# Expert layers of a two-layer decoder: one gather and one residual write per group of eight experts, where there was one per four

## The chip, the cores and the metric

The kernel runs on one core of one Trainium2 chip. The metric is the device time of one execution in microseconds (us), of which the median over runs is taken. The engines are named as the profile names them: PE (matrix products), DVE and ACT (elementwise work), POOL, and SP, which here issues nearly all transfers. Transfers from memory run on the core's 16 DMA engines.

## What is computed

The reference is a trunk of two layers over 528 rows (16 meta tokens and 512 tokens) of width 1024, in float32. Layer 0 is a gated short convolution, layer 1 latent attention, and behind each stands a mixture of experts, added to the residual `h`:

```
grp    = argmax(xf @ w_grp)                      # one of 8 groups per token
top_i  = the best 2 of the group's 8 experts     # 64 experts in all
gate   = p_group * p_expert / sum(p_expert)
hh     = silu(xb @ w_gate[e]) * (xb @ w_up[e])   # 1024 -> 256
ys     = hh @ w_down[e]                          # 256 -> 1024
y      = sum over a token's two experts of ys * gate
h      = h + y
```

Each expert has three matrices of 1 MB (1024x256, 1024x256, 256x1024), so a layer's 64 experts are 192 MB of weights, and every one is read once.

## The kernel before

**Quads.** The experts of a layer are taken four at a time. Such a *quad* (16 a layer, 0 to 15) has 128 slots, 32 for each expert (`CAP`), which lie on the 128 partitions; two quads make a group. `Moe.run` walks over the quads, and `quad` (L663) writes the PE's work out by hand in this order:

- `gate_up(q, gu, xT, 0)` and `(…, 1)` (L573): the four experts' gate products and up products, 64 PE records each, with `combined` of the quad before it between and behind them (L667, L671);
- `gather` for the quad to come (L532): a 0/1 matrix `dr` that `select_scaled` builds on DVE (slots by tokens, times the row's norm) multiplies `h`, in float32: 5 token tiles (4 in layer 1, which has no meta tokens) times two halves of 512 columns;
- `scatter` (L552): a small product that tells each slot its token and its gate;
- `turn` (L582): silu on ACT, a product on DVE, two transposes; `turned` (L543): eight transposes of the gathered rows, which give `xT` of the next quad;
- `down` (L594): the down products in two halves; `split_scaled` (L213) puts gate times result into a high and a low part, and `combine_part` (L645) multiplies both by the 0/1 matrix `DT` (tokens by slots, from `back`, L565) and adds the product to `h`, tile by tile, on DVE (L651).

The first gather of a layer is another: `first_gather` (L419) makes `xT` straight away with `h` as the stationary operand, eight products of 128 columns for each token tile.

**The ring.** All weights come through one ring of 1 MB slots (`Ring`, L67). The order of the loads is fixed, SP issues them one by one, and each waits until the slot's former load was released: `gate_up` releases four slots a call, `down` four. Slots are of four kinds: A (4), B (5 in layer 0, 9 in layer 1, `NB`), K and R together (13 and 10, `NR`), and X (3 and 4, `NX`). K and R, on the right of the memory, serve loads up to the first of quad `LATE` (12 in layer 0, 15 in layer 1). At that quad `late_work` (L653) gives their memory up, runs a loop for experts with over 32 tokens (its count is zero for these inputs; the engines jump over it), starts what is wanted for the next stage (in layer 1 the load and spreading of the last norm's weights, L1272 to L1276), and opens the X slots.

So the order is set by hand on PE, by the ring on SP, and by the scheduler, which follows the order of the calls, on DVE and ACT.

## Time and profile before

| what | value |
|---|---|
| median of 3 runs | 1456.99 us (1456.9 to 1458.02) |
| the profiled execution's own time | 1459.79 us |
| its span, first to last instruction | 1458.0 us |
| PE busy | 1349.8 us, 93% |
| DVE, ACT busy | 661.4 us, 305.0 us |
| data moved | 438.14 MB, mean 301 GB/s |

The span holds five stages: the convolution layer and first routing (to 265 us), the experts of layer 0 (265 to 750), attention (750 to 986), the experts of layer 1 (986 to about 1445), and the last norm with the output. In the page's digits each place is a fortieth of the span (36.45 us), 9 is 90% or more. A wait counts where it stands ahead of the instruction that ends last; a busy PE may be working on something whose end nobody waits for yet.

### The profile page before, as it was taken

Reading aid. Unit: us, or ns where it says so; the run is one execution under the profiler, and the core shown is the slowest. Engines: PE = TensorE matmul, PEld = TensorE weight load, DVE = VectorE, ACT = ScalarE, POOL = GpSimd, SP = SyncE. Lnnn points to the kernel's source line nnn. Section 1 sums busy time; section 2 is a strip of 40 time slices with the busy share of each in tenths; the row PEclk is TensorE's granted clock in tenths of the full one; section 3 lists DMA queues with packets and bytes.
Section 4 is the critical chain, followed back from the end, with each engine's and each line's share of the span. In section 5 each row is a group of like instructions: output and inputs, shape, how many; then the busy total and the mean of one; then the engine's idle time right before and its main releaser. Section 6 shows DMA issues by size and latency. Waiting matters only on the chain. (4 is left out here: it accounts for less than half of the span.)

```text
span 1458.0 us, 23499 instructions
## 1 busy us (share of the span) xinstructions
PE 1349.8 (93%) x9847; PEld 843.9 (58%) x9847; DVE 661.4 (45%) x1495; ACT 305.0 (21%) x665; POOL 50.6 (3%) x131
## 2 busy tenths in 40 slices
PE   6999999999999999988989999999999989888966
PEld 6999758644444444433458888895454444443422
DVE  4555325444344434443455676544444433433334
ACT  6333112100101000120134675421111100101002
POOL 1011101000000000000011000000000000000001
PEclk9999998999999999999999999999999999999987
DMA  8322534699999999479950002968999999999982
GB/s 300 145 89 95 228 146 174 248 414 416 420 420 419 420 420 419 182 290 423 416 212 26 30 30 87 363 252 340 419 419 419 419 419 419 419 419 419 419 322 81
DMA packets 66854, 438.14 MB, mean 301 GB/s; under 512 B 8353, under 2 KB 8737, under 8 KB 16178
## 3 DMA queue, kind: packets, MB, share of 16 engines
q1 hardware_dynamic: 65008, 435.79, 73.5%
q8 instruction: 81, 1.33, 0.4%
q10 hardware_dynamic: 1730, 0.74, 0.2%
q14 instruction: 35, 0.29, 0.1%
HBM read 434.40 MB, written 2.10 MB: 299 GB/s over the span
## 5 line engine op out<-in xcount | busy, mean ns | idle before, releaser
L539 PE MATMUL w<-h,dr 128*128 128x512 f32 x480 | 218.0, 602 | 0.0
L651 DVE TENSOR_TENSOR h<-h,w 128x512 f32<-128x512 f32 x256 | 158.9, 682 | 122.7 <-PE w L649 122.7
L649 PE MATMUL w<-y,DT 128*128 128x512 f32 x576 | 166.5, 423 | 7.4 <-ACT y L214 3.4
L539 PEld LDWEIGHTS w<-h,dr 128*128 128x128 f32 x480 | 87.5, 190 | 116.4 <-issue 105.9
L577 PE MATMUL gu<-B,xT 128*32 128x256 f32 x1456 | 129.4, 400 | 20.6 <-issue 12.7
L649 PEld LDWEIGHTS w<-y,DT 128*128 128x128 f32 x576 | 90.8, 179 | 82.8 <-DVE h L651 31.6
L577 PE MATMUL gu<-R,xT 128*32 128x256 f32 x1648 | 124.0, 386 | 4.5 <-DMA R<-in_w_up_dram 3.7
L214 ACT ACTIVATE y<-dn,gs 128x512 fp32r<-128x512 f32 x64 | 44.0, 688 | 363.8 <-PE w L649 202.5
L522 DVE TENSOR_TENSOR dr<-rm,cs 128x640 f32<-128x640 f32 (+1 forms) x30 | 22.7, 758 | 191.7 <-PE w L539 191.7
L577 PEld LDWEIGHTS gu<-B,xT 128*32 128x32 f32 x1456 | 62.9, 115 | 65.1 <-issue 31.6
L577 PE MATMUL gu<-A,xT 128*32 128x256 f32 x640 | 82.5, 405 | 17.1 <-DMA A<-in_w_up_dram 11.6
L540 ACT ACTIVATE xg<-w 128x512 f32<-128x512 f32 x60 | 35.9, 598 | 277.7 <-PE w L539 277.7
L577 PEld LDWEIGHTS gu<-R,xT 128*32 128x32 f32 x1648 | 63.1, 111 | 47.3 <-issue 12.4
L867 PE MATMUL acc<-xH,wL 128*128 128x264 f32 x384 | 79.0, 286 | 0.0
L867 PE MATMUL acc<-xL,wH 128*128 128x264 f32 x384 | 78.3, 284 | 0.2 <-DVE xL L211 0.2
L867 PE MATMUL acc<-xH,wH 128*128 128x264 f32 x384 | 78.1, 284 | 0.1
L585 DVE TENSOR_TENSOR sg<-sg,gu 128x256 f32<-128x256 f32 x32 | 13.5, 421 | 134.6 <-ACT sg L584 134.6
L215 DVE SCALAR_TENSOR_TENSOR y<-dn,gs,y 128x512 fp32r<-128x512 f32 x64 | 47.7, 746 | 53.6 <-ACT y L214 53.5
L606 PE MATMUL dn<-A,sg 128*32 128x512 f32 x272 | 67.7, 674 | 2.9 <-DVE sg L591 2.9
L606 PE MATMUL dn<-R,sg 128*32 128x512 f32 x344 | 63.4, 682 | 2.9 <-DVE sg L591 2.8
L214 ACT ACTIVATE wH<-A,gc 128x256 fp32r<-128x256 f32 (+1 forms) x119 | 52.7, 521 | 61.7 <-PE acc L867 37.0
L577 PEld LDWEIGHTS gu<-A,xT 128*32 128x32 f32 x640 | 38.5, 117 | 44.3 <-DMA A<-in_w_up_dram 15.4
(348 smaller groups left out, 2154.7 us busy)
## 6 DMA issues: line engine op xcount, KB each, us to landing
R<-in_w_up_dram SPq DMA_DIRECT2D x55, 1024.0 KB, 19.9
B<-in_w_gate_dram SPq DMA_DIRECT2D x51, 1024.0 KB, 19.9
R<-in_w_gate_dram SPq DMA_DIRECT2D x48, 1024.0 KB, 19.9
R<-in_w_down_dram SPq DMA_DIRECT2D x43, 1024.0 KB, 14.1
B<-in_w_up_dram SPq DMA_DIRECT2D x40, 1024.0 KB, 19.8
A<-in_w_down_dram SPq DMA_DIRECT2D x32, 1024.0 KB, 18.1
B<-in_w_down_dram SPq DMA_DIRECT2D x31, 1024.0 KB, 19.9
A<-in_w_up_dram SPq DMA_DIRECT2D x22, 1024.0 KB, 19.9
```

Source lines behind the costliest of these rows:

```text
L214: i = A.activation(H, src, AF.Copy, scale=g)
L215: return i, V.scalar_tensor_tensor(L, src, g, H.bitcast(F32), op0=ALU.mult, op1=ALU.subtract)
L522: V.tensor_tensor(d.rearrange("p t (e s) -> p t e s", e=4), self.rm0[:, :, 4 * q:4 * q + 4, None].to_broadcast([P, nT, 4, CAP]), iota(1, C ...
L539: T.matmul(ps, dr[:n, t], h[t][:n, 512 * u:512 * u + 512], start=t == 0, stop=t == nT - 1)
L540: A.activation(xg[:, :, 64 * u:64 * u + 64], ps.rearrange("s (p k) -> s k p", k=8), AF.Copy)
L577: T.matmul(gu[CAP * e:CAP * e + CAP, s, :256], xT[k // 4][:, k % 4, CAP * e:CAP * e + CAP], w[e][:, k], start=k == 0, stop=k == 7)
L585: V.tensor_tensor(sg, sg, gu[:, 1, :256], op=ALU.mult)
L606: T.matmul(dn[CAP * e:CAP * e + CAP, :n], hT[:, b, CAP * e:CAP * e + CAP], w[:, b, c:c + n], start=b == 0, stop=b == 1)
L649: T.matmul(ps[:m, :n], DT[:, P * t:P * t + m], a, start=i == 0, stop=i == 1)
L651: V.tensor_tensor(hh, hh, ps[:m, :n], op=ALU.add)
L867: T.matmul(ps[:, u, :HALF], l[:, k, P * m:P * m + P], r[:, k, HALF * u:HALF * u + HALF], start=k == 0 and l is wH and r is xH, stop=k == 7 ...
```

## The change

A group's tokens (up to 128) are gathered once, unscaled and in token order, when its first quad is prepared (`gather` in every odd quad, for two quads); the norm is applied when ACT copies them out. Each quad then picks its slots from those rows: `choose` builds a 0/1 matrix `sel` (tokens of the group by slots) and `select` multiplies it with the gathered rows, which takes the place of the eight transposes. The quad's results, copied out unscaled, are multiplied by the transposed and gated `sel` (`combine`), in float32, and summed over the two quads of a group in two PSUM banks `yg`. Once a group, in the even quad that follows, `yg` is split (`parts`) and spread to the tokens (`spread`), half by half, with the add to `h`. Layer 0 and 1 end differently: the last quad goes to `h` by itself (`last_down`). Moreover the ring of layer 1 has 8 B slots and not 9, and `late_work` of layer 1 comes at quad 12 and not at 15.

```diff
-NA, NB, NR = 4, (5, 9), (13, 10)
+NA, NB, NR = 4, (5, 8), (13, 10)
-LEFT = range(5), (0, 1, 8, 2, 4, 3, 5, 6, 7)
+LEFT = range(5), (0, 1, 2, 4, 3, 5, 6, 7)
-LATE = 12, 15
+LATE = 12, 12
...
+        def gather_tile(self, ps, t, first, last):
+            n, d = rows(t), self.d[:rows(t), t].bitcast(F32)
+            for u in range(2):
+                i = T.matmul(ps[u], d, h[t][:n, 512 * u:512 * u + 512], start=first, stop=last, skip_group_check=True)
+            return i
...
+        def choose(self, q, ag):
+            sel = self.ep.tile([P, 4, CAP], F32, tag="sel", name="sel", bufs=2)
+            V.tensor_tensor(sel, ag[:, 4 * (q % 2):4 * (q % 2) + 4, None].to_broadcast([P, 4, CAP]),
+                            iota(1, CAP)[:, None, :].to_broadcast([P, 4, CAP]), op=ALU.is_equal)
...
+        def select(self, q, xT, bank):
+            for u in range(2):
+                ps = bank().rearrange("p (k s) -> p k s", k=4)
+                for k in range(4):
+                    T.matmul(ps[:, k], self.xg[:, 4 * u + k], self.sel[q], start=True, stop=True)
+                V.tensor_tensor(xT[u], ps, self.g8[:, 4 * u:4 * u + 4, None].to_broadcast([P, 4, P]), op=ALU.mult)
+            return xT
...
         def first_gather(self, psum):
-                for u in range(2):
-                    for k in range(4):
-                        i = T.matmul(ps[u][:, k], chunk8(t, 4 * u + k), self.dr[:n, t], start=first and k == 0, stop=last,
+                T.matmul(pa[:, :10], self.d[:n, t].bitcast(F32), self.aux[:n, t, :10], start=first, stop=last)
+                i = self.gather_tile(ps, t, first, last)
...
+            self.scaled_tokens(ps, self.ag0)
+            self.choose(0, self.ag0)
+            self.select(0, self.x0, bank)
...
+                def gather(g):
+                    d, ag = self.new_d(), self.new_ag()
+                    V.tensor_tensor(d, self.rm0[:, :, NE + g, None].to_broadcast([P, nT, P]),
+                                    iota(1, P)[:, None, :].to_broadcast([P, nT, P]), op=ALU.is_equal)
+                    pa = bank()
+                    for t in tiles:
+                        n = rows(t)
+                        T.matmul(pa[:, :18], d[:n, t].bitcast(F32), self.aux[:n, t], start=t == 0, stop=t == nT - 1)
+                    V.tensor_copy(ag, pa[:, :18])
+                    ps = [bank(), bank()]
+                    for t in tiles:
+                        self.gather_tile(ps, t, t == 0, t == nT - 1)
+                    self.scaled_tokens(ps, ag)
+                    return ag
...
+                def turn_slots(q):
+                    ps = bank()
+                    T.transpose(ps[:, :P], self.sel[q], ident)
+                    A.activation(self.sel[q], ps[:, :P], AF.Copy)
...
+                def down(q, hT):
+                    y = self.wk2.tile([P, 2, 512], F32, tag="xy", name="y")
+                    for u in range(2):
+                        A.activation(y[:, u], down_part(q, hT, u, 0, 512 * u, 512), AF.Copy)
+                    return y
...
+                    for u in range(2):
+                        T.matmul(self.yg[:, u], self.sel[q], y[:, u], start=q % 2 == 0, stop=q % 2 == 1 or q == 14)
...
+                def parts(u):
+                    y = self.wk2.tile([P, 2, 512], F32R, tag="xy", name="yHL")
+                    split(y[:, 0], y[:, 1], self.yg[:, u])
+                    return y
...
+                def spread_part(y, DT, t, c0, n):
                     m = rows(t)
+                    ps = bank()
                     for i, a in enumerate(y):
                         T.matmul(ps[:m, :n], DT[:, P * t:P * t + m], a, start=i == 0, stop=i == 1)
                     hh = h[t][:m, c0:c0 + n]
                     V.tensor_tensor(hh, hh, ps[:m, :n], op=ALU.add)
...
+                def quad(q, xT, y):
+                    ends = y is not None and (q % 2 == 0 or q == 15)
...
                     gate_up(q, gu, xT, 0)
+                    if y is not None:
+                        combine(q - 1, y)
+                    if ends:
+                        half = parts(0)
                     gate_up(q, gu, xT, 1)
...
+                    if ends:
+                        DT = back(self.agp[:, 8:9])
+                        spread(half, DT, 0)
+                    ag = self.ag
+                    if q % 2 and q < 15:
+                        ag = gather(q // 2 + 1)
                     if q < 15:
-                        xg = gather(select_scaled(q + 1))
+                        self.choose(q + 1, ag)
+                    if q > 0 and q < 15:
+                        turn_slots(q)
+                    if ends and q == 15:
+                        spread(parts(1), DT, 1)
...
                     hT = turn(gu)
+                    if q == 15:
+                        return last_down(q, hT, tg[:, 1:2], DT)
+                    xT = self.select(q + 1, self.new_x(), bank)
...
+                    if ends:
+                        spread(parts(1), DT, 1)
+                    y = down(q, hT)
...
                     if q == LATE[layer]:
                         with tc.manual_schedule(engines={ET.PE}):
-                            for f in left[1:]:
-                                f()
-                        left = ()
+                            combine(q - 1, y)
+                            spread_all()
+                        y = None
                         late_work()
```

The one-hot of a gather and the matrix of the spread share one buffer `d`, and `y` and both halves of the split share one buffer `xy`.

**PE, layer 0, from the last up product of quad 1 to its down products, before:** `dr` is the 0/1 matrix, `hm` the meta tile, `xg` the gathered rows.

```order
L649 MATMUL w<-y,DT 128x512 x8
L649 MATMUL w<-y,DT 16x512 x2
L539 MATMUL w<-h_63,dr 128x512
L539 MATMUL w<-h_64,dr 128x512
L539 MATMUL w<-h_65,dr 128x512
L539 MATMUL w<-h_66,dr 128x512
L539 MATMUL w<-hm,dr 128x512
...
L556 MATMUL misc<-aux,d_2931 128x10 x5
L589 MATMUL misc<-cs,sg 128x128 x2
L548 MATMUL w<-cs,xg 128x128 x8
```

Every quad has these rows (the five of L539 twice). In the changed kernel the same place stands as follows in an odd quad (1):

```order
L561 MATMUL w<-aux,d 128x18 x5
L431 MATMUL w<-h_63,d 128x512 x2
L431 MATMUL w<-h_64,d 128x512 x2
L431 MATMUL w<-h_65,d 128x512 x2
L431 MATMUL w<-h_66,d 128x512 x2
L431 MATMUL w<-hm,d 128x512 x2
L608 MATMUL w<-cs,sel 128x128
L596 MATMUL w<-cs,sg 128x128 x2
L450 MATMUL w<-sel,xg 128x128 x8
```

And in an even quad (4):

```order
L651 MATMUL w<-yHL,d 128x512 x8
L651 MATMUL w<-yHL,d 16x512 x2
L608 MATMUL w<-cs,sel 128x128
L596 MATMUL w<-cs,sg 128x128 x2
L450 MATMUL w<-sel,xg 128x128 x8
L651 MATMUL w<-yHL,d 128x512 x8
L651 MATMUL w<-yHL,d 16x512 x2
```

The gather moved to the odd quads, the writes to the residual (L651) to the even ones, and L450 stands where the transposes stood; in every quad L634, two products of 512 columns, now comes between gate and up.

**SP, layer 1, around the loop that is jumped over**, of the changed kernel (L680 reads the count, L778 is the loop's branch):

```order
L101 DMA B_11242<-in_w_down_dram 128x2048
L101 DMA A_11281<-in_w_down_dram 128x2048
L101 DMA A_11283<-in_w_down_dram 128x2048
L680 TENSOR_LOAD wl
L778 COMPARE_AND_BRANCH
...
L101 DMA X_12103<-in_w_gate_dram 128x2048
L101 DMA X_12105<-in_w_gate_dram 128x2048
L101 DMA X_12107<-in_w_gate_dram 128x2048
L101 DMA X_12109<-in_w_gate_dram 128x2048
```

Before, the loop stood behind the fifth of the eight half loads of quad 15's down weights, and only the last three of them went to X slots; now it stands behind the last load of quad 12, and quad 13 begins in the X slots.

## Rows read from the trace of the kernel before

**Rows 1.** The page: PE's total, granted clock and DMA in 40 slices.

```profile
PE 1349.8 (93%) x9847; PEld 843.9 (58%) x9847; DVE 661.4 (45%) x1495; ACT 305.0 (21%) x665; POOL 50.6 (3%) x131
...
PEclk9999998999999999999999999999999999999987
DMA  8322534699999999479950002968999999999982
```

**Rows 2.** Busy time by stage: length, engines with instruction counts, clock, DMA share, GB/s.

```profile
292.00:583.00 291.00, 282.30 (x2073) 130.73 (x2074) 126.38 (x239) 28.88 (x49) 0.00 (x0) 0.96 1.01 419
583.00:636.00 53.00, 45.23 (x382) 21.28 (x375) 20.26 (x36) 4.33 (x7) 0.00 (x0) 0.94 0.50 199
636.00:738.00 102.00, 93.58 (x669) 44.27 (x665) 46.71 (x93) 17.02 (x32) 0.00 (x0) 0.93 0.97 396
...
1156.00:1404.40 248.40, 214.34 (x1668) 106.45 (x1661) 91.59 (x175) 24.35 (x41) 0.00 (x0) 0.97 1.01 419
...
990.00:1408.00 418.00, 374.22 (x3022) 188.32 (x3014) 166.12 (x326) 45.64 (x76) 0.00 (x0) 0.98 1.01 418
```

**Rows 3.** Timeline, PE alone, quad 11 of layer 0: start, length, line, form, [idle before].

```profile
584.96 3.63 PE L577 MATMUL gu<-R,xT 128*32 128x256 f32 x64
588.51 2.76 PE L649 MATMUL w<-y,DT 128*128 128x512 f32 x10
591.20 3.66 PE L577 MATMUL gu<-R,xT 128*32 128x256 f32 x64
...
597.62 3.70 PE L539 MATMUL w<-h,dr 128*128 128x512 f32 x8
601.25 1.12 PE L539 MATMUL w<-hm,dr 16*128 16x512 f32 x2
...
606.98 0.81 PE L556 MATMUL misc<-aux,d 128*128 128x10 f32 x5
...
608.28 0.48 PE L589 MATMUL misc<-cs,sg 128*128 128x128 f32 x2 [0.49 <-DVE gs L561]
608.59 1.04 PE L548 MATMUL w<-cs,xg 128*128 128x128 f32 x8
...
610.05 5.32 PE L606 MATMUL dn<-R,sg 128*32 128x512 f32 x32 [0.42 <-DVE sg L591]
```

**Rows 4.** One line's instructions: SP's last loads of quad 11's up weights.

```profile
L101 SPq DMA_DIRECT2D R<-in_w_up_dram x2: 328/356/384, 555.3 to 555.7; - x2
...
DMA to landing us min/median/max: 13.6/13.6/13.6
```

**Rows 5.** Timeline, layer 0 at quad 12, where the loop is jumped over.

```profile
619.85 2.51 PE L649 MATMUL w<-y,DT 128*128 128x512 f32 x9 [0.52 <-DVE y L215]
...
624.48 2.00 SPq L101 DMA_DIRECT2D X<-in_w_down_dram  x3
627.92 5.18 PE L577 MATMUL gu<-A,xT 128*32 128x256 f32 x64 [5.55 <-issue]
```

**Rows 6.** PE's waits, 1156 to 1404.4 us: total, times, longest.

```profile
PE gu L577 <- DMA A<-in_w_up_dram: 11.6, 8, 1.9
```

**Rows 7.** SP's last load of quad 15's up weights, layer 1.

```profile
L101 SPq DMA_DIRECT2D A<-in_w_up_dram x1: 328/328/328, 1387.9 to 1387.9; - x1
...
DMA to landing us min/median/max: 19.9/19.9/19.9
```

**Rows 8.** Timeline, layer 1 from the jump at quad 15 on.

```profile
1417.10 3.62 PE L577 MATMUL gu<-B,xT 128*32 128x256 f32 x26 [12.70 <-issue]
...
1420.66 3.78 PE L1275 MATMUL dn<-gf,one_f 1*128 1x512 f32 x4
...
1444.66 0.69 ACT L214 ACTIVATE y<-dn,gs 128x512 fp32r<-128x512 f32 x1 [2.30 <-PE dn L606]
```

**Rows 9.** Timeline, PE, the end of the first gather of layer 0.

```profile
259.56 5.48 PE L427 MATMUL acc<-dr,h 128*128 128x128 f32 x22
```

**Rows 10.** Timeline, PE, up products of quad 7 in layer 1.

```profile
1167.04 5.02 PE L577 MATMUL gu<-B,xT 128*32 128x256 f32 x58 [1.89 <-DMA B<-in_w_up_dram]
```

More of the change, by code (lines that the diff above doesn't have):

```diff
@@ L349, in prepare @@
             self.done = []
+            G.tensor_copy(self.aux[:, :, 8], tok1[:, :nT])
             if nT == 5:
@@ L513, in run @@
                 ring.open([B[i] for i in LEFT[layer]], limit)
[L514 to L517 removed]
+                for a in ("gup", "psm", "ygp") if layer == 0 else ("psm", "gup", "ygp"):
                     setattr(self, a, pool(st, f"{a}{layer}", space=PSUM))
@@ L532, in gather @@
-                def gather(dr):
-                    xg = self.wk2.tile([P, 8, P], F32, tag="xy", name="xg")
-                    for u in range(2):
-                        ps = psum.tile([P, 512], F32, tag="w", name="w", bufs=3)
-                        for t in tiles:
-                            n = rows(t)
-                            T.matmul(ps, dr[:n, t], h[t][:n, 512 * u:512 * u + 512], start=t == 0, stop=t == nT - 1)
-                        A.activation(xg[:, :, 64 * u:64 * u + 64], ps.rearrange("s (p k) -> s k p", k=8), AF.Copy)
-                    return xg
@@ L543, in turned, with bank @@
[L543 to L553 removed]
+                def bank():
+                    return psum.tile([P, 512], F32, tag="w", name="w", bufs=3)
@@ new lines, in gather, with back @@
+                    V.tensor_copy(ag, pa[:, :18])
[4 more added lines that the diff above has]
+                    return ag
+                def back(tok):
+                    tk = self.wk2.tile([P, 5], F32, tag="tk", name="tk")
+                    V.tensor_scalar(tk, off5, tok, None, op0=ALU.add)
+                    DT = self.new_d().rearrange("p t c -> p (t c)")[:, :self.ntok]
@@ new lines, in down_part @@
+                def down_part(q, hT, u, key, c, n):
+                    dn = self.dnp.tile([P, 512], F32, tag="dn", name="dn", bufs=2)
+                    for b in range(2):
+                        for e in range(4):
+                            w = ring.get(("d", layer, q, key, e))
+                            T.matmul(dn[CAP * e:CAP * e + CAP, :n], hT[:, b, CAP * e:CAP * e + CAP], w[:, b, c:c + n],
+                                     start=b == 0, stop=b == 1)
+                    if c + n == w.shape[2]:
+                        for e in range(4):
+                            ring.release(("d", layer, q, key, e))
+                    return dn
@@ new lines, in down, with combine @@
+                def down(q, hT):
[3 more added lines that the diff above has]
+                    return y
+                def combine(q, y):
+                    if q % 2 == 0:
+                        self.yg = self.ygp.tile([P, 2, 512], F32, tag="yg", name="yg")
+                    for u in range(2):
+                        T.matmul(self.yg[:, u], self.sel[q], y[:, u], start=q % 2 == 0, stop=q % 2 == 1 or q == 14)
+                    del self.sel[q]
@@ L646, in combine_part, with spread @@
+                def parts(u):
+                    y = self.wk2.tile([P, 2, 512], F32R, tag="xy", name="yHL")
+                    split(y[:, 0], y[:, 1], self.yg[:, u])
+                    return y
+                def spread(y, DT, u):
+                    for t in order:
+                        spread_part([y[:, 0], y[:, 1]], DT, t, 512 * u, 512)
+                def spread_part(y, DT, t, c0, n):
                     m = rows(t)
-                    ps = psum.tile([P, 512], F32, tag="w", name="w", bufs=3)
+                    ps = bank()
@@ L651, in combine_part, with last_down @@
                     V.tensor_tensor(hh, hh, ps[:m, :n], op=ALU.add)
+                def last_down(q, hT, gs, DT):
+                    held = []
+                    for u, (c0, c1) in enumerate(LAST[layer]):
+                        n = c1 - c0
+                        dn = down_part(q, hT, u, u, 0, n)
+                        y = self.wk2.tile([P, 2, 512], F32R, tag="xy", name="yHL")
+                        y = [y[:, i, :n] for i in range(2)]
+                        i, _ = split_scaled(*y, dn[:, :n], gs)
+                        if held:
+                            with behind(i):
+                                for t, v in held:
+                                    done(t, v)
+                        for t in order:
+                            spread_part(y, DT, t, c0, n)
+                        if done is not None:
+                            m = 2 if u == 0 else len(order)
+                            for t in order[:m]:
+                                done(t, u)
+                            held = [(t, u) for t in order[m:]]
                 def late_work():
@@ new lines, in quad @@
+                    hT = turn(gu)
+                    if q == 15:
+                        return last_down(q, hT, tg[:, 1:2], DT)
+                    xT = self.select(q + 1, self.new_x(), bank)
+                    if q == 14:
+                        self.tg = self.wk2.tile([P, 2], F32, tag="tg", name="tg")
+                        ps = bank()
+                        T.matmul(ps[:, 0:1], self.sel[15], ag[:, 8:9], start=True, stop=True)
+                        V.tensor_copy(self.tg[:, 0:1], ps[:, 0:1])
```

207 lines of the change are left out of this document (66 added, 141 removed).

## The prediction

> **What bounds the kernel now.** I read the digits by slice first, then the stages, then the timeline of one quad, then SP's loads. By the totals PE is the bound: it is busy 93% [rows 1]. But in the same slices in which PE shows 9, from the eighth to the sixteenth and from the 29th on, the DMA digits show 9 too [rows 1], and the table by stage says how full that is: 419 GB/s from 292 to 583 us and 418 from 990 to 1408 [rows 2], with no gap. A quad's weights are twelve loads of 1024 KB, 12.58 MB; at 419 GB/s that is 30.0 us a quad. So the experts have two bounds that lie close together, and what a faster PE is worth is what PE lags behind the weights.
>
> In layer 0 PE takes 30.4 us for quad 11, from its first gate product at 584.96 to the end of its down products at 615.37 [rows 3]; the mean over quads 0 to 11 is (615.4 − 265.0) / 12 = 29.2 us, 265.0 being the end of the first gather [rows 9]. PE is thus hardly faster than the transfers and keeps the lag that it got at the start. How long the lag is: the last up weights of quad 11 were issued at 555.7 and landed 13.6 us later, at 569.3 [rows 4]; the up products that use them end at 594.86 [rows 3], where 569.3 + 3.66 = 573 would have done. **The lag is 22 us.** In layer 1 PE has no meta tile and has caught up long before: from 1156 to 1404 it is busy 214.3 of 248.4 us while the DMA is full [rows 2], and the largest of its waits are for up weights, none longer than 1.9 us since loads land one by one [rows 6]. There PE's work is covered, down to the last quad.
>
> Two places are bound by neither. At quad 12 of layer 0 PE ends at 622.36 and restarts at 627.92 with nothing to wait for but the jump over the loop [rows 5], and transfers fall to 199 GB/s around it, since the K and R slots are out and the X slots not yet in [rows 2]. At quad 15 of layer 1 the same jump costs 12.70 us of PE [rows 8], after all up weights were there: the last was issued at 1387.9 and landed at 1407.8 [rows 7]. What follows runs partly at half clock, and 3.78 us of it is the spreading of the norm's weights [rows 8].
>
> **PE's work in a quad.** Removed: a gather of 2 × (3.70 + 1.12) = 9.64 us in every second quad, and of the writes to `h` (2.76 us for a half with five tiles) two halves in every second quad [rows 3]. Added: `combine`, two float32 products of 512 columns, four records of which eight take 3.70, so 1.85; one transpose of `sel`, 0.13 (an eighth of 1.04). The table look-up of 0.81 now comes once in two quads [rows 3]. Replaced: eight transposes at 1.04 by `select`, eight float32 products of 128 columns. Its price is not in the trace. It has two records for each product where a transpose has one, so 2 × 1.04 = 2.1 from below; from above, 22 records of the first gather, the same form with a strided stationary operand, take 5.48, so sixteen take 4.0 [rows 9]. The gathered rows lie contiguous, as the transposes read them, and I take 2.1.
>
> - Even quad: 3.63 + 1.85 + 3.66 + 2.76 + 0.6 + 2.1 + 2.76 + 3.6 (down at full clock) = 21.0.
> - Odd quad: 3.63 + 1.85 + 3.66 + 0.81 + 9.64 + 0.6 + 2.1 + 3.6 = 25.9.
> - Two waits of 0.4 to 0.5 stand in each quad now [rows 3]; ACT's copy of the gathered rows before `select` and the handing over of the `w` banks add to that. I allow 1.5 a quad.
>
> The mean is 24.9 against 29.2, 4.3 less. But 24.9 is under 30.0, so after 22 / 4.3, some five quads, PE has eaten the lag and waits for weights. ACT and DVE do less than before and had room (661 and 305 us busy of 1458 [rows 1]); what they add, the one-hot matrices and the splits of `yg`, is hidden by the gate and up products, except where I count it.
>
> **Layer 0 up to the loop.** The first gather costs PE 4.0 us a tile now and 1.85 + 0.2 after; the last tile no longer waits behind a train of 22 records, but a chain of copy, `choose` and `select` follows it, about 4 us. I take 2 earlier (0 to 4). The transfers start with PE's first release, so they move by 2 as well, and are full from there: the up weights of quad 11 land at 567.3. Then 3.66 up, 0.81 and 9.64 for the next group, 1.0 of waits, 0.6 and 2.1, 3.6 down: 588.7. `combine` with its copy, 2.6; a split, 0.69 on ACT [rows 8] and as much on DVE, 1.4; half the spread, 2.76; the second split cannot start before the first half is read, since both use `xy`, 1.4; 2.76: 599.6. Before it was 622.36 [rows 5]. **Gain 22.5** (PE must have kept 24.9 or so; bounds 12 and 26).
>
> **Layer 0 from the loop on.** Twelve slots serve three quads, and transfers run at 396 GB/s from 636 to 738 [rows 2], 5.6 us short of full. Up weights of quad 13 wait for slots that the down products of quad 12 release; these come some 7 us sooner without a gather ahead of them, so up to 5.6 can be won. Against it, in quad 15 both halves of the spread (5.5) and a split (1.4) now stand between the last up and the last down products. I take 1 net (−2 to 5). Layer 0: 23.5. Attention is untouched and PE-bound, so all of it is handed on.
>
> **Layer 1.** The stream of weights is full from the first release to the last load, so PE's savings are worth nothing before the last quad. Three things move its end: the first gather, 2 earlier (0 to 4); one ring slot less, so one load more after the start, 2.5 later; and the loop at quad 12. There SP comes to the loop early, behind a load whose slot the gate products of quad 11 release, and waits in front of the X slots. In layer 0 the X loads went out 2 us after PE's last product [rows 5], before the jump was over. With 19.9 us from issue to landing [rows 7], eight loads of 2.5 us in flight, this pause is covered if the X slots come in time; PE's pause of 12.70 is covered by the next 30 us of weights. I take 1 later (0 to 12). The last up weights then land at 1407.8 − 2 + 2.5 + 1 = 1409.3.
>
> From there: up, 3.66 at full and 5.02 at partly halved clock [rows 10], taken as 4.3; spread, split, spread with four tiles, 2.2 + 1.4 + 2.2; gate column, transposes and their copies 1.5; half of down, 1.85; split 1.4; spread 2.2; half of down 1.85: 1428.2. Before, the copy behind the last down products starts at 1444.66 [rows 8]. I take 2 off for products at half clock: **gain 14.5**. The 13.3 us of norm and output behind stay.
>
> **Sum.** 23.5 + 14.5 = 38 us of the profiled span of 1458.0, so 1420.0. That execution took 1459.79 with what lies around the span, 2.8 above the median of the runs shown, 1456.99; from the median 38 lead to **1419 us**.
>
> **Rivals.**
> *The loop in layer 1 stalls the stream.* The jump took 5.55 us where transfers were half idle and 12.70 where they ran [rows 5, 8]; now it comes amid full ones. If the X slots wait for it, or it takes 25, the loads in flight run out and each further us is lost: some 12, 1431. Against it: SP stands ahead of PE. 15%.
> *PE keeps less.* If `select` costs 4.0 and the waits 3 a quad, the mean is 28.3, the lag shrinks by 0.9 a quad, 10 of 22 are won in layer 0: 1431. Layer 1 stays. 10%.
> *The clock falls.* PE waits more often now, and after a wait of 1.89 the up products of quad 7 took 5.02 [rows 10]. Inside a quad the 5 us of cover take that. On the two chains behind the last up weights, 20 us each with some 14 of products, half clock throughout costs about 14 in all, 2 of it counted: 1431. The Trainium skill (TensorE: Matmul & The Clock Gate, section HAM oscillation) says that a kernel whose products between two transfers are shorter than the wait for the next one starts every stretch at the low clock, and so speaks against this change. The trace agrees in part: from 1156 to 1404, with waits in every quad, the mean clock is still 0.97 [rows 2], and by the row I leave it at 2 us. 10%.
> *Better.* All of the 5.6 after the loop, a first gather 4 earlier twice, no loss of clock: 1407. 10%.
> *Slower.* One buffer `d` for one-hot and spread, one `xy` for results and both halves of the split, three `w` banks for all: if each hand-over holds PE, with DVE's adds between, a quad may take 8 us more, 32.9, over the transfers' 30.0. Then sixteen quads take 526, against 481 in layer 0 and 459 in layer 1 (265 to 746, 986 to 1445): 1569. It decides from some 6.5 us a quad on, where the excess over 30.0 in 28 quads eats the 38. Against it: the splits lie behind 3.6 us of other products each, and the two hand-overs that a quad has now cost 0.9 us together [rows 3]. 4%.
> That the change does less than it says is out: the order of PE shows the gather in odd quads alone.
>
> **How the numbers follow.** The forecast's own case has 51%, 1412 to 1426; the three middle cases 35%, 1424 to 1438, of which I give 2 to all of them together, which ends near no change; better 10%, slower 4%. A range of **1404 to 1439** leaves out the slow case and the far ends of the others, under 2 in 10. Faster by over 0.2% (some 3 us, what a measurement can tell here) 0.94, within 0.02, slower 0.04.
>
> **What would show it.** Right: L431 with 14 gathers of ten or eight products; PE waiting for weights from quad 5 or 6 of layer 0 on; the loop of layer 0 near 600; transfers full from 270 to 585, and in layer 1 through quad 12; 19 us from the last up weights to the last down products. Wrong: PE in layer 0 over 28 us a quad without waits for DMA, a hole in the transfers of layer 1 at quad 12, or `select` over 4 us.

## The result and the profile after

The changed kernel takes **1417.51 us** (median of 4 runs, 1416.4 to 1418.74) against 1456.95 (4 runs, 1454.75 to 1458.02): a ratio of **0.9731, 95% interval 0.9715 to 0.9748**, 39.4 us less. The forecast was 1419.0 in a range of 1404 to 1439. The profiled execution took 1416.49, its span is 1414.7, 43.3 less than the span of before; of these, 3.8 lie in the two profiled executions, of which the one of before stood 2.8 above its median and this one 1.0 below.

The page after, the totals and the digits that answer to [rows 1]:

```profile
PE 1252.2 (89%) x9647; PEld 791.2 (56%) x9647; DVE 517.0 (37%) x1238; ACT 311.0 (22%) x708; POOL 49.3 (3%) x138
...
PEclk9999999999999999889999999999999999997999
DMA  8322464699999999899930012959999999998995
```

The stages after, to be read beside [rows 2] (length, busy time of PE, PEld, DVE, ACT, POOL, then clock, DMA share, GB/s):

```profile
283.00:560.00 277.00, 247.08 (x2013) 121.89 (x2013) 71.64 (x145) 29.93 (x59) 0.00 (x0) 0.96 1.01 420
560.00:605.00 45.00, 37.13 (x253) 18.95 (x257) 12.14 (x24) 4.32 (x8) 0.00 (x0) 0.89 0.86 348
605.00:714.00 109.00, 86.81 (x707) 41.62 (x701) 37.94 (x76) 17.73 (x36) 0.19 (x1) 0.94 0.96 390
...
1270.00:1310.00 40.00, 24.18 (x151) 10.42 (x153) 10.12 (x17) 2.39 (x4) 0.00 (x0) 0.74 0.88 357
```

Ahead of the loop of layer 0 the transfers are as full as before (420 GB/s) and PE is no longer (247 of 277 us, where it was 282 of 291): the weights now set the pace in both layers. The fourth row is new: in layer 1, at quad 12, the transfers fall to 357 GB/s. That hole in the transfers is one of the things that the prediction named as a sign of being wrong.

PE after, quad 11 of layer 0, for [rows 3 and 5] (`<-issue` marks a wait for nothing that the profile shows):

```profile
550.35 5.94 PE L584 MATMUL gu<-R,xT 128*32 128x256 f32 x58 [1.73 <-DMA R<-in_w_gate_dram]
...
560.33 3.64 PE L584 MATMUL gu<-R,xT 128*32 128x256 f32 x58 [1.56 <-DMA R<-in_w_up_dram]
...
565.22 7.13 PE L431 MATMUL w<-h,d 128*128 128x512 f32 x16
...
589.83 2.50 PE L651 MATMUL w<-yHL,d 128*128 128x512 f32 x9 [0.56 <-DVE yHL L211]
597.42 3.20 PE L584 MATMUL gu<-A,xT 128*32 128x256 f32 x26 [5.09 <-issue]
```

The up products start the moment the last up weights land, 560.3, where PE lagged 22 us; the gather comes in the odd quad; PE is through at 592.33 (before 622.36) and restarts at 597.42 (before 627.92). The gate products of this quad took 5.94 and not 3.6: after waits of 1.7 to 1.9 us part of them runs at half clock, which costs nothing while PE waits for weights anyway.

Layer 1 after, where the loop now stands: PE, SP's loads, and SP's waits from 1240 to 1330 us (total, times, longest):

```profile
1281.93 2.01 PE L651 MATMUL w<-yHL,d 128*128 128x512 f32 x7 [0.49 <-DVE yHL L211]
1297.68 0.64 PE L584 MATMUL gu<-A,xT 128*32 128x256 f32 x2 [13.73 <-DMA A<-in_w_down_dram]
```

```profile
1274.48 2.81 SPq L101 DMA_DIRECT2D A<-in_w_down_dram  x2
1297.64 2.10 SPq L101 DMA_DIRECT2D X<-in_w_gate_dram  x4
```

```profile
SPq L778 <- DMA B<-in_w_down_dram: 7.3, 2, 4.8
SPq L778 <- SPq L778: 6.5, 3, 2.5
...
SPq L778 <- DMA A<-in_w_down_dram: 5.0, 2, 2.5
```

The last load ahead of the loop, issued at 1277.0, lands 19.9 us later, at 1296.9. SP stands at the loop's branch until then, landing by landing; the last events at L778 stand at 1297.1 to 1297.3 on all five engines; the X loads leave at 1297.64 and PE starts again at 1297.68. So **who enters the loop waits for every load on the way**, on all engines, and behind it the transfers start from nothing.

The trace of before had shown such waits, in rows that the prediction did not read: SP at its loop (L725) in layer 0, from 590 to 630 us, and in layer 1, from 1400 to 1420:

```profile
SPq L725 <- DVEq L725: 24.5, 1, 24.5
```

```profile
SPq L725 <- DMA B<-in_w_down_dram: 8.0, 1, 8.0
```

In layer 0 it stood there until DVE had come to the loop too, in layer 1 for a load.

The end of layer 1, from the last up weights on:

```profile
1382.24 0.40 PE L584 MATMUL gu<-A,xT 128*32 128x256 f32 x1 [1.21 <-DMA A<-in_w_up_dram]
...
1385.82 2.33 PE L651 MATMUL w<-yHL,d 128*128 128x512 f32 x8
1388.84 0.50 PE L651 MATMUL w<-yHL,d 128*128 128x512 f32 x1 [0.69 <-ACT yHL L210]
...
1393.88 1.92 PE L616 MATMUL dn<-X,sg 128*32 128x512 f32 x16 [1.09 <-DVE sg L598]
```

The down products end at 1401.3, 19.1 behind the last up weights. Before, the copy behind them started at 1444.66 [rows 8], 36.9 behind.

**Where the 43.3 us of the span come from**, place by place: the first gate products of layer 0 start at 256.1 and not 265.0, 8.9; from there to the loop 21.2; the rest of layer 0, to its last down products, 1.2; from there to the first gate products of layer 1, 1.7, which is put down to its first gather; the experts of layer 1, from the first gate to the last down product 448.4 in place of 458.7, 10.3.

### The profile page after: what moved, and what is told of

The parts are those of the page before. It is cut to its first block, busy times and chain, and to the rows that moved or that the text cites. A ratio compares the mean times of both kernels' runs of the same rounds, so it can differ in the third digit from the quotient of the medians.

```text
span 1414.7 us, 22875 instructions
## 1 busy us (share of the span) xinstructions
PE 1252.2 (89%) x9647; PEld 791.2 (56%) x9647; DVE 517.0 (37%) x1238; ACT 311.0 (22%) x708; POOL 49.3 (3%) x138
## 4 chain that ended last, share of the span: by engine, by line
DMA 31%; PE 22%; DVE 3%; ACT 1%; issue 1%; SPq 0%; POOL 0%; DVEq 0%; ACTq 0%; POOLq 0%
DMA B<-in_w_gate_dram 6%; DMA R<-in_w_down_dram 4%; DMA B<-in_w_up_dram 4%; PE gu L584 3%; DMA R<-in_w_up_dram 3%; DMA A<-in_w_up_dram 3%; DMA A<-in_w_gate_dram 3%; DMA X<-in_w_up_dram 3%; DMA A<-in_w_down_dram 3%; PE a L1030 2%; PE sc L1193 2%; PE pj L1287 2%; PE acc L290 2%; DMA K<-in_w_down_dram 1%; DMA B<-in_w_down_dram 1%; PE dn L616 1%
## 5 line engine op out<-in xcount | busy, mean ns | idle before, releaser
L584 PE MATMUL gu<-B,xT 128*32 128x256 f32 x1392 | 145.4, 430 | 30.5 <-DMA B<-in_w_gate_dram 22.2
L584 PE MATMUL gu<-A,xT 128*32 128x256 f32 x736 | 106.8, 448 | 34.6 <-DMA A<-in_w_down_dram 13.7
L651 PE MATMUL w<-yHL,d 128*128 128x512 f32 (+1 forms) x324 | 95.4, 424 | 11.5 <-ACT yHL L210 3.4
L431 PE MATMUL w<-h,d 128*128 128x512 f32 x224 | 99.7, 598 | 0.0
L653 DVE TENSOR_TENSOR h<-h,w 128x512 f32<-128x512 f32 x144 | 89.5, 681 | 6.7 <-PE w L651 6.4
L651 PEld LDWEIGHTS w<-yHL,d 128*128 128x128 f32 (+1 forms) x324 | 50.0, 178 | 52.9 <-DVE h L653 16.6
L626 ACT ACTIVATE y<-dn 128x512 f32<-128x512 f32 x60 | 35.8, 597 | 192.4 <-PE dn L616 185.2
L450 PE MATMUL w<-sel,xg 128*128 128x128 f32 x480 | 64.3, 291 | 4.5 <-ACT xg L436 4.5
L431 PEld LDWEIGHTS w<-h,d 128*128 128x128 f32 x224 | 41.4, 190 | 47.1 <-issue 46.4
L450 PEld LDWEIGHTS w<-sel,xg 128*128 128x128 f32 x480 | 60.3, 204 | 7.2 <-ACT xg L436 7.2
L920 PEld LDWEIGHTS acc<-xL,wH 128*128 128x128 f32 x384 | 60.5, 190 | 0.2 <-DVE xL L211 0.2
L920 PEld LDWEIGHTS acc<-xH,wH 128*128 128x128 f32 x384 | 60.1, 191 | 0.8 <-ACT wH L214 0.5
## 6 DMA issues: line engine op xcount, KB each, us to landing
R<-in_w_down_dram SPq DMA_DIRECT2D x48, 1024.0 KB, 19.9
R<-in_w_up_dram SPq DMA_DIRECT2D x47, 1024.0 KB, 19.9
R<-in_w_gate_dram SPq DMA_DIRECT2D x44, 1024.0 KB, 19.9
B<-in_w_down_dram SPq DMA_DIRECT2D x35, 1024.0 KB, 19.9
A<-in_w_down_dram SPq DMA_DIRECT2D x28, 1024.0 KB, 19.9
A<-in_w_gate_dram SPq DMA_DIRECT2D x26, 1024.0 KB, 19.9
```

Source lines behind the costliest of these rows:

```text
L431: i = T.matmul(ps[u], d, h[t][:n, 512 * u:512 * u + 512], start=first, stop=last, skip_group_check=True)
L450: T.matmul(ps[:, k], self.xg[:, 4 * u + k], self.sel[q], start=True, stop=True)
L584: T.matmul(gu[CAP * e:CAP * e + CAP, s], xT[k // 4][:, k % 4, CAP * e:CAP * e + CAP], w[e][:, k], start=k == 0, stop=k == 7)
L626: A.activation(y[:, u], down_part(q, hT, u, 0, 512 * u, 512), AF.Copy)
L651: T.matmul(ps[:m, :n], DT[:, P * t:P * t + m], a, start=i == 0, stop=i == 1)
L653: V.tensor_tensor(hh, hh, ps[:m, :n], op=ALU.add)
```

## The experiments

All medians are of 4 runs (5 in one case); the kernel before, run beside them, had medians from 1456.86 to 1457.96, so two or three us between kernels of different groups are little. "The change" is 1417.51.

### What the weights cover

```diff
...
                 for k in range(4):
-                    T.matmul(ps[:, k], self.xg[:, 4 * u + k], self.sel[q], start=True, stop=True)
+                    for _ in range(2 if q else 1):
+                        T.matmul(ps[:, k], self.xg[:, 4 * u + k], self.sel[q], start=True, stop=True)
```

and the same with 4.

> The changed kernel with every product of select issued twice in the 30 quads that have one (same values written again). Select takes 2.05 us a quad in the trace of the change, so PE does 30 x 2.05 = 61 us more. Theory (the weights set the pace, 30.0 us a quad; the gain of layer 0 was the 22 us by which PE lagged, and that is all eaten by quad 5): PE needs some 26.5 a quad instead of 24.4 and still catches up, by quad 7 or so; only the few selects behind the last up weights count: +2 to +5, 1420 to 1423. Rival (the time follows PE's work): +61, some 1478. In the trace the theory wants PE waiting for up weights from quad 7 or 8 of layer 0 on, and transfers still at 420 GB/s.

> The changed kernel with every product of select issued four times: 6.15 us of PE more a quad, 185 in all. Theory: PE needs 30.5 a quad in layer 0, just over the 30.0 of the weights, so the lag is never eaten: the loop of layer 0 comes some 30 later (366 us for twelve quads from 256), its last four quads a few us later, and layer 1, which has no meta tile, stays near the pace of the weights and gives 0 to 10: +30 to +50, 1447 to 1467. Rival (the time follows PE's work): +185, 1602. If twice costs next to nothing and four times costs +30 or more, the cover is the 5 us a quad of the prediction.

Measured: twice **1423.43** (ratio 0.9762, 0.9746 to 0.9778), four times **1439.44** (0.9878, 0.9849 to 0.9908). The costliest groups, `select` in the change and in the two (count, busy us, mean ns):

```profile
L450 PE MATMUL w<-sel,xg 128*128 128x128 f32 x480 | 64.3, 291 | 4.5 <-ACT xg L436 4.5
```

```profile
L451 PE MATMUL w<-sel,xg 128*128 128x128 f32 x960 | 121.7, 289 | 4.5 <-ACT xg L436 4.5
```

```profile
L451 PE MATMUL w<-sel,xg 128*128 128x128 f32 x1920 | 224.0, 278 | 4.5 <-ACT xg L436 4.5
```

57 us more of PE's work cost 5.9, a little over the +2 to +5 that were expected; 160 us more cost 21.9, well under the +30 to +50. The rival is out. PE's waits of the first of the two, 260 to 600 us:

```profile
PE gu L585 <- DMA R<-in_w_up_dram: 9.7, 6, 1.9
PE gu L585 <- DMA R<-in_w_gate_dram: 3.9, 2, 2.0
```

With four times, PE waits for no weights there at all. It then takes 29.05 us a quad (the down products of quads 5 and 11 end at 426.7 and 601.0), under the 30.5 that was expected: four selects took 7.5 us a quad (90.0 us for twelve) where 8.2 were counted, and the clock was 0.99 of full where the change has 0.96. So the lag shrinks by 1 a quad, and the loop comes 18.8 later than in the change. Layer 1 alone took 451.7 against 448.4: 3 us for some 80 us of added products. Both layers thus cost less than the expectation had.

### The first gather of layer 0

```diff
...
                 i = self.gather_tile(ps, t, first, last)
+                if self.layer == 0:
+                    for k in range(4):
+                        i = T.matmul(jk[:, P * k:P * k + P], chunk8(t, k), self.d[:n, t].bitcast(F32), start=first and k == 0, stop=last,
+                                     skip_group_check=True)
```

> The changed kernel with four more products of 128 columns for each token tile in the first gather of layer 0, of the old form (h as the strided stationary operand), into a bank that nobody reads; 8 records of 0.25 us a tile, 2.0, so that a tile costs PE about what it did before. Theory (PE is busy without a gap from 236 us to the first gate products, so every tile's products delay the routing of the next, and the 8.9 us by which the first gate products came earlier are PE work of all five tiles): they come 8 to 10 us later, and the kernel takes +7 to +10, 1425 to 1427. Rival (the prediction: only the last tile's train lies on the path): +2 to +4. Rival (the gain came from the shorter routing on DVE): 0 to +1.

Measured: **1437.17** (0.9862, 0.9846 to 0.9878), 19.7 more, above every expectation. The gate products start at 268.73, 12.6 later. The granted clock told more than the sum of the products: it fell to half in this stretch, as it had in the kernel before. So the added products of the meta tile were left out:

```diff
-                if self.layer == 0:
+                if self.layer == 0 and t != META:
...
```

> As first_train, but without the four added products of the meta tile (16 rows deep); those of the four token tiles stay, 8 records of 0.25 us a tile, 8.0 us in all. In first_train the first gate products came 12.6 us later (268.7, from 256.1), and PE's clock stood at half from 243.6 to 253.8; in the kernel before it stood at half from 238.0 to 248.2, also while PE went through the meta tile's products; in the change's own profile it did not fall there. Theory (of the 12.6, 5.1 are the half clock, and what let it fall are the shallow products of the meta tile): no or little half clock before the first gate products, which come at 262 to 264; +8 to +11 in all, 1426 to 1429. Rival (the clock falls there whenever PE is busy for so long without a gap): 10 us at half clock, gate products at 267, and a time within 3 us of first_train, 1434 to 1440.

Measured: **1427.71** (0.9801, 0.9785 to 0.9817), in the range of the theory. The stretch from 235 to 250 us in the kernel before, in the change, in this run and in `loop_late_l1` below, whose code is that of the change up to layer 1 (columns as above; in the run with the meta tile's products the clock from 235 to 257 was 0.77):

```profile
235.00:250.00 15.00, 15.00 (x78) 13.77 (x79) 6.60 (x34) 2.59 (x6) 1.28 (x3) 0.66 0.86 350
```

```profile
235.00:250.00 15.00, 15.00 (x90) 10.30 (x89) 10.52 (x49) 3.28 (x10) 1.07 (x4) 1.00 0.86 350
```

```profile
235.00:250.00 15.00, 15.00 (x89) 11.25 (x88) 10.30 (x48) 3.27 (x10) 0.92 (x3) 1.00 0.84 345
```

```profile
235.00:250.00 15.00, 15.00 (x80) 11.39 (x80) 8.10 (x37) 2.78 (x8) 1.19 (x5) 0.77 0.87 350
```

PE is busy without a gap in all four. A mean of 0.66 over 15 us is 10.2 us at half clock (1.2 in place of 2.4 GHz), worth 5.1 if all that PE did then took twice its time. By this estimate, of the 8.9 us of the first gather **about 5.1 are the clock and 3.8 PE's work**. That the work of every tile counts is shown by this run: at full clock the gate products came at 261.67, 5.6 later for 8 us of added products, more than the rival of the last tile alone gives (2 to 4). With the meta tile's products they came 7.1 later still.

What let the clock fall is not shown. The changed kernel's own first gather has products of 16 rows too. In six of the ten traces that have it without added products (`after`, `sel_four_times`, `no_loop`, `loop_14_l0`, `early_spread`, `early_spread_gather`) the clock stayed full there and the gate products came at 254.9 to 256.1. In four (`sel_twice`, `loop_late_l1`, `nine_slots`, `early_all_nine`) it stood at half for some 7 us, in `loop_late_l1` from 239.6 to 246.4, and they came at 258.5 to 259.4. One trace without a fall does not tell the shallow products from this spread. In both traces with the code of before (`before`, `before_loop_12`) it fell, and they came at 265.0 and 265.6. So the change gains here in either case, but how much of the 5.1 it gets differs from one execution to the next.

Of the 10.2 us that `train_no_meta` takes more, 4.6 lie in the experts of layer 0, 3.1 of them behind the loop. There runs of the same code differ by up to 6.7 (from PE's restart to the last down products 117.4 us in the change, 124.1 in `loop_late_l1`); what that is stays open.

### The loop in layer 1

Back to quad 15 (with the lines for its last token numbers taken out of the branch on `ends`), out altogether, and the kernel before with the loop at quad 12:

```diff
-LATE = 12, 12
+LATE = 12, 15
...
-                    if ends and q == 15:
-                        spread(parts(1), DT, 1)
+                    if q == 15:
+                        if ends:
+                            spread(parts(1), DT, 1)
```

> The changed kernel with the loop of layer 1 at quad 15 again. Theory (entering the loop waits until every load that was issued has landed, on all engines, and the pause lies behind the last up weights again): the hole of 5.4 us in the transfers at quad 12 is gone, so the last up weights land some 5 earlier; behind them PE pauses 12 to 13 and the spreading of the norm's weights, 2 to 4, comes on the path: +7 to +12, 1425 to 1430. Rival (where the loop stands doesn't matter, layer 1 gained by PE's work): 0 within 2. The prediction's own numbers: +13 for the pause, 3 to 4 for the spreading, less 1 for a loop at quad 12: +15.

```diff
-                    with tc.issue_after(ring.last.ins):
-                        self.nover = nc.values_load(self.wl[:, NE:NE + 1], min_val=0, max_val=NE)
-                    self.overflow(psum)
```

> The changed kernel without the loop for experts with over 32 tokens, in both layers (what it leaves out: those experts; with these inputs its count is zero). Theory (entering the loop waits for all loads on the way): in layer 1 the X loads no longer wait for quad 12's last down load to land; they go out as soon as the K and R slots of quad 11 are free, the hole of 5.4 us is gone or down to 1 or 2, and PE's pause of 13.7 shrinks to what the X slots' handing over costs; in layer 0 PE's pause of 5.1 and about as much of the hole there go: -5 in layer 1 and -3 to -6 in layer 0, 1406 to 1410. Rival (the prediction: SP gets ahead and only PE pauses at the jump): -1 in layer 1 and -5 in layer 0, 1411 to 1413, with the X loads no earlier against the landing of the loads before them.

```diff
-LATE = 12, 15
+LATE = 12, 12
```

> The kernel before with one line of the change alone: the loop of layer 1 at quad 12 (nine B slots stay). Theory (in layer 1 PE's work is covered, its gain comes from the loop alone): layer 0 as before; in layer 1 the pause of 12.7 and the 3.8 of the norm's weights leave the tail and a hole of some 5 comes into the transfers: -8 to -13, 1444 to 1450. Rival (layer 1's gain comes from PE's lighter quads, the loop's place matters little): 0 to -3, and PE's pause at quad 12 is added to a PE that has only 3 us a quad to catch up.

Measured: at quad 15 **1424.97** (0.9771, 0.9755 to 0.9788); without the loop **1407.82** (0.9657, 0.9639 to 0.9675); before with the loop at 12 **1443.97** (0.9909, 0.9887 to 0.9931). All three lie where the theory put them, two of them at its edge, and outside the rivals. SP without the loop, at the place where it had stood:

```profile
1270.11 2.81 SPq L101 DMA_DIRECT2D A<-in_w_down_dram  x2
1275.07 7.78 SPq L101 DMA_DIRECT2D X<-in_w_gate_dram  x4
```

The X loads follow the others without a pause. From the first gate product of layer 1 to the last up weights it takes 423.9 us without the loop and 429.4 with it at quad 12: **the hole costs 5.5**. In layer 0 the experts take 455.4 without the loop and 458.7 with it, a difference within the spread of runs of the same code there. At quad 15 it costs the end of the kernel instead (PE, its profiled execution, which took 1434.9, 10 over its median; 11.9 of what it takes over the change lie ahead of layer 1):

```profile
1395.11 0.64 PE L584 MATMUL gu<-A,xT 128*32 128x256 f32 x2 [10.49 <-issue]
...
1398.66 3.78 PE L1329 MATMUL dn<-gf,one_f 1*128 1x512 f32 x4
```

Layer 1 takes 455.0 there, 442.9 without the loop, 448.4 in the change. And in the kernel before, with the loop at quad 12:

```profile
1329.01 0.64 PE L577 MATMUL gu<-A,xT 128*32 128x256 f32 x2 [17.98 <-DMA A<-in_w_gate_dram]
...
1409.94 3.64 PE L577 MATMUL gu<-B,xT 128*32 128x256 f32 x58 [1.18 <-DMA B<-in_w_up_dram]
```

PE stands for 18 us, and its heavier quads catch that up all the same. Layer 1 takes 441.8, less than in the change: 426.1 to the last up weights (nine slots), and 15.7 from there, where the change needs 19.1. **In layer 1 the loop's move alone gives more (16.9) than the whole change (10.3)**. The rest gives some back: 3.3 ahead of the last up weights, where the change has one ring slot less, and 3.4 behind them, where it has both halves of a group's spread.

### The ring slot, and the loop of layer 0

```diff
-NA, NB, NR = 4, (5, 8), (13, 10)
-LEFT = range(5), (0, 1, 2, 4, 3, 5, 6, 7)
+NA, NB, NR = 4, (5, 9), (13, 10)
+LEFT = range(5), (0, 1, 8, 2, 4, 3, 5, 6, 7)
...
-            eq = rp.tile([P, 8, 8], F32, tag="eq", name="eq", bufs=1)[:n]
...
+            eq = se
             V.tensor_tensor(eq, s8[:, None, :].to_broadcast(sh), s8[:, :, None].to_broadcast(sh), op=ALU.is_equal)
...
-            om = small("om", 8)
+            om = ex
```

> The changed kernel with nine B slots in layer 1 again; the 352 bytes a partition that it lacks are found by letting two scratch tables of the routing lie in others that are done with. Theory (one load more is on the way ahead of layer 1's stream): the last weights land 2.5 earlier, -2 to -3, 1415. Rival (the stream is paced by its rate from PE's first release and the hole at quad 12 is the same): 0 within 1.

Measured: **1420.79** (0.9734, 0.9708 to 0.9759), nothing gained. From the first gate product to the last up weights of layer 1 it took 427.0, 2.3 less, as priced; but in its profiled execution the last chain took 21.3 (down products at half clock) and the routing of layer 0 fell to the low clock. What the slot is worth is not settled by this run.

```diff
-LATE = 12, 12
+LATE = 14, 12
```

> The changed kernel with the loop of layer 0 at quad 14 instead of 12 (and the weights of the latents loaded behind quad 14). The hole in layer 0's transfers, from 570 us to the first X landing at 606, moves behind two more quads. If what follows the hole is bound by the transfers, as from 605 to 705 (390 GB/s), its place changes nothing there, and the later split of the latents' weights may cost: 0 to +5. If the slots that are there at quad 14 hold a larger part of what is left, PE works through the hole: -5 to -15. I think the second the likelier: 1405 to 1413.

Measured: **1423.34** (0.977, 0.9748 to 0.9791), some 6 slower; the case thought likelier was wrong. In its trace SP's pause ahead of the X loads is shorter (from 640.36 to 653.65, where in the change it is from 572.83 to 595.18), but the transfers behind it are less full, 348 GB/s from 656 to 720 us where the change has 390 from 605 to 714. Layer 0 takes 462.1 in it, against 458.7; why it is not faster stays open.

### A version that beats both

In the last quad `combine`, both halves of the spread and the table of the quad's own tokens go ahead of the up products, `combine` and the first split ahead of the gate products too:

```diff
+                    if q == 15:
+                        combine(q - 1, y)
+                        half = parts(0)
                     gate_up(q, gu, xT, 0)
...
+                    if q == 15:
+                        gate_slots(q, self.ag)
+                        if ends:
+                            DT = back(self.agp[:, 8:9])
+                            spread(half, DT, 0)
+                            spread(parts(1), DT, 1)
...
+                        gate_up(q, gu, xT, 1)
+                        return last_down(q, turn(gu), tg[:, 1:2], DT)
```

> The changed kernel with the last quad of both layers reordered on PE: combine of quad 14 and the first split ahead of quad 15's gate products, both halves of the spread ahead of its up products, so that behind the last up weights only up, turn and down with the quad's own spread are left. Theory (the two chains behind the last up weights, 19 to 21 us each, end the two layers, and PE waits for weights ahead of them): of some 7 us that leave a chain 2 to 4 come back because PE reaches the up products later than the weights land, or because the last down load lands only 11 us behind the last up load: -3 to -5 in each layer, 1408 to 1412. Rival (the end is set by the landing of the last down loads): 0 to -2.

To this, in layer 0, the gather of quad 11 ahead of its up products:

```diff
...
+                    if q == early:
+                        ag = gather(q // 2 + 1)
...
```

> As early_spread, and in layer 0 the gather for quads 12 and 13 ahead of the up products of quad 11, where PE waits for weights, in place of behind them: 10.5 us of PE less between the last up weights of quad 11 and the loop. Theory (the hole from 570 to 606 us in layer 0 is closed by the first X load, which waits for PE's last product and the loop): the loop comes 5 to 9 earlier; of that layer 0 keeps about as much as it kept of the 15 us by which the X loads came earlier without the loop, 3.3: -2 to -4 beside early_spread. Rival (behind the loop the slots pace the transfers, the hole's length counts for nothing): 0 within 1.

and the nine slots:

> As early_spread_gather, with nine B slots in layer 1 and the two shared scratch tables as in nine_slots. In nine_slots layer 1 from its first gate product to the last up weights took 427.0, 2.4 less than in the change (429.4), while the median stayed the same. Theory (the slot is worth 2.4, and that run's routing fell to the low clock): -2 to -3 beside early_spread_gather. Rival (the shared scratch tables cost in the routing what the slot gives): 0 within 1.

Measured: **1402.56** (0.9636, 0.962 to 0.9652), **1403.98** (0.9641, 0.9625 to 0.9658) and **1399.59** (0.9607, 0.9591 to 0.9623). The first is worth 15 us, more than expected: layer 0 takes 450.5 from first gate to last down product (458.7 in the change), layer 1 441.3 (448.4). The gather's move gives nothing (1.4 more). PE there, quad 11:

```profile
558.93 7.13 PE L431 MATMUL w<-h,d 128*128 128x512 f32 x16
566.00 1.98 PE L431 MATMUL w<-hm,d 16*128 16x512 f32 x4
567.91 3.66 PE L584 MATMUL gu<-R,xT 128*32 128x256 f32 x64
```

The up weights had landed at 559.5: the gather only stands ahead of other work now, and the loop is reached 1 us earlier. The best of all has all three; the nine slots give it 4.4 beside the second, where 2 to 3 were expected, and in its trace layer 1 takes 439.8 where the second has 442.5. The end of its layer 1:

```profile
1367.21 2.25 PE L651 MATMUL w<-yHL,d 128*128 128x512 f32 x8
...
1373.30 3.95 PE L584 MATMUL gu<-B,xT 128*32 128x256 f32 x64
...
1378.19 0.51 PE L596 MATMUL w<-cs,sg 128*128 128x128 f32 x2 [0.93 <-DVE sg L592]
```

The spread lies ahead of the up products, whose weights land at 1373.6; the last down products end at 1386.6, 13.0 later.

## Why the prediction was right

- **The bound.** "What a faster PE is worth is what PE lags behind the weights" held: the lag was taken as 22 us, PE went over to waiting at quad 5, as forecast, and from the first gate product to the loop 21.2 were won, where the sum had 20.5 (22.5 less 2 for the first gather). From the last up weights of quad 11 to PE's last product ahead of the loop it took 32.0, where the prediction had worked out 32.3. `sel_twice` and `sel_four_times` show the other side of the same sentence.
- **`select`** took 2.1 us a quad (64.3 us for 30 quads), as taken from below.
- **The first gather of layer 0 was sized wrong**: 2 (0 to 4), measured 8.9. The step that failed is "the last tile no longer waits behind a train": PE is busy throughout, so the work of all tiles counts, by estimate 3.8, which the bounds held; and the clock, which stood at half for 10.2 us before, did not fall in the profiled execution, by estimate 5.1. That second part is luck: the rival on the clock had looked only for a fall in the changed kernel, not for one in the kernel before, and in four other traces of the changed first gather it does fall. In layer 1 the same step gave 1.7, near the 2.
- **The loop of layer 1 was wrong in its mechanism**: "SP comes to the loop early", "this pause is covered if the X slots come in time", "I take 1 later (0 to 12)". It cost 5.5, since entering the loop waits for all loads on the way, and no X load can leave before. "SP stands ahead of PE", given against the rival, is no protection: it was SP that waited, as it had at the loops of the kernel before (24.5 and 8.0 us). The rival "the loop in layer 1 stalls the stream" was right in kind, at less than half its price, and the prediction's own sign of it, the hole at quad 12, was there.
- **The tail of layer 1** was worked out as 18.9 behind the last up weights, to which the sum added 2 for the clock; it is 19.1, so the 2 were not needed in this execution (in that of `nine_slots`, 21.3). The slot, taken as 2.5, agrees with the 2.3 of `nine_slots` from first gate to last up weights.
- **The clock inside the quads** fell often for parts of a quad and cost little, as left in the sum: the gate products of quad 11 took 5.94 in place of 3.64 behind waits of 1.9 and 1.7 us, while the mean from 283 to 560 us is 0.96. The Trainium skill (TensorE: Matmul & The Clock Gate, section HAM oscillation) says that a kernel whose products between two transfers are shorter than the wait for the next one starts every stretch at the low clock. That condition is not met here: PE is busy 247 of 277 us, with no wait over 1.9, and the mean agrees with that.
- **Three readings were loose**, though no term goes by them. The DMA's digits show 9 from the ninth slice on, not the eighth. PE's show 8 in the 15th, 16th and 33rd and from the 35th to the 37th. And the pause of 12.70 at quad 15 began at 1404.4, ahead of the landing of the last up weights at 1407.8.
- **The sum** of 38 came out near the 39.4 partly by luck. In the profiled pair the places add up to 43.3, of which 3.8 are where the two executions stood against their medians. Against the sum, the first gather gave 6.9 more, the tail 1.8 more, the rest of the terms 0.6 more; the loop and the slot together took 7.5 where 3.5 were set. Misses that point opposite ways left a good total.

## What to carry to other kernels

Where transfers and an engine lie close together, measure the engine's lag behind the landings at the last place that counts. That lag, not the work removed, is what a lighter engine can win; and work put ahead of the last landing costs little as long as the engine still waits for landings there, where the same work behind the last landing is paid in full. Before a loop or a branch is moved into a full stream, ask which transfers its entry waits for: the waits at the loop as it stands may already tell. And a stretch whose engine is 100% busy may still run at the low clock: read the clock of the kernel before, not only of the change, and in more than one execution.

## What the runs showed of the hardware that was not expected

- The clock of PE fell to half while PE was busy without a gap (from 238.0 to 248.2 us in the kernel before, for some 7 us in four of ten traces of the changed first gather, not at all in the other six). Products of 16 rows depth stand ahead of that place in all of these traces; what lets the clock fall is open.
- More work raised the clock: with `select` four times, the mean over the profiled run was 0.986 against 0.959; from 260 to 600 us PE waited for no weights there.
- The entry of a loop whose count is zero held all engines until the last load on the way had landed: 13.7 us of PE, 5.5 us of the stream.
